# Sums of activations beside five column tiles, buffers allocated ahead, and a head's side work in one sequence, in a two-layer hybrid encoder

## The chip, the cores and the metric

The kernel runs on one core of one Trainium2 chip. The metric is the device time of one execution in microseconds (us); before the change the median of three runs is 1840.49 us (1838.7 to 1841.06). One more execution, taken by the hardware profiler, is the source of all rows quoted here.

A core has five engines that run side by side, each with its own queue in order: TensorE (PE; its weight loads are listed as PEld), VectorE (DVE), ScalarE (ACT), GpSimd (POOL) and SyncE (SP), which here issues most of the DMA transfers. TensorE writes to PSUM, eight banks of 512 float32 columns for each of 128 partitions; all else lies in SBUF or in DRAM.

## The reference

Sixteen learned meta tokens are put ahead of 512 tokens of width 2048, and two layers follow, each `h <- h + post_norm(mixer(pre_norm(h)))`. Layer 0 is softmax attention (16 query heads, 8 key heads, rotary positions). Layer 1, where the change lies, is gated linear attention (GLA) in two directions:

```python
def gla_mixer(h, w_in, gk_up, gk_bias, o_norm, w_out):
    ...
    proj = hp @ w_in
    q, k, v, g_out, lr_f, lr_b = jnp.split(proj, [s1, s2, s3, s4, s5], axis=-1)
    ...
    o_f = gla_chunked(q, k, v, log_gate(lr_f, gk_up[0], gk_bias[0]), strict=False)
    o_b = flip(gla_chunked(flip(q), flip(k), flip(v), ..., strict=True))
    o = (o_f + o_b).transpose(0, 2, 1, 3)[:, pad:]
    o = rmsnorm(o, o_norm).reshape(B, L, GLA_VALUE_DIM)
    return (o * jax.nn.silu(g_out[:, pad:])) @ w_out
```

It has 4 heads with keys of width 256 and values of width 512. `w_in` has the columns 0 to 1023 for q, 1024 to 2047 for k, 2048 to 4095 for v, 4096 to 6143 for the gate `g_out`, and 32 for the two low-rank decay gates. All is float32.

## The kernel before

**Three products for one.** Every float32 operand is split into a rounded part and the rest (`split`, L133 to L135: ScalarE casts to `hi`, VectorE subtracts to get `lo`), and a product is `hi*hi + hi*lo + lo*hi`: three matmuls (L157 to L159, L242 to L244). Activations lie as `uh`, `ul` (16 blocks of 128 rows, 528 columns, the tokens). `weights` (L146 on) loads a unit of 8 x 128 columns of weights into one of two `wraw` buffers through SP and splits it into one of three pairs `whi`, `wlo`. `project` takes two units, 16 blocks, and one or two column ranges of tokens (`HALVES` is twice 264, `REAL` is 512), accumulates in one of three PSUM banks of the tag `pp`, and hands the bank to an evacuation function.

**The order of the work** is that of the Python program, worked out as it runs: a small planner, `Clock`, has a time of its own that each projection block advances (`clk.step`) and a heap of side tasks with due times (`clk.after`, generators through `clk.drive`; `clk.finish` runs tasks until the named ones are done, whether or not projections go along). A framework below it adds the waits, assigns buffers, and moves instructions ahead where `high_priority` says so (weights by 400 instructions, quarters of `seven` by 600). Each engine then runs its list in that order.

**The stages around the change**, in order of time:

- *Residual and second norm.* After the attention layer, `residual` builds the new `h`, stores it in DRAM as `hf_d`, and writes the next layer's `uh`, `ul`. `second_norm` (L844) turns sums of squares of each token into a row `r1row` (one value for each token, the same in all partitions): for each of five groups of tokens it puts the values on a diagonal (`dg`, VectorE), multiplies by a matrix of ones (TensorE, `mrow`) and copies the result to its columns of `r1row` (ScalarE). `mrow` has one PSUM bank. Two `pp` banks hold the low-rank products `plr` until `r1row` has come.
- *Column tiles that go through DRAM.* `to_dram(n, c, ...)` (L858) projects 128 columns of `w_in`, multiplies by `r1row` and stores the tile in `kq_d[n]`: n = 0, 1 are the k tiles of head 0, n = 2 is its first q tile.
- *Sums of activations.* `combine` (L198) runs as a side task beside n = 1 and n = 2. For each k of 8 it loads block k and block k + 8 of `hf_d` into a buffer `x` of four times 264 columns, scales them by the norm's weights (L210, L211), forms the four combinations T1 to T4 by three subtractions (L212 to L214), and splits the result into `th`, `tl`. There are four buffers `x` (`quarters`).
- *Value tiles by seven products.* `seven` (L219) computes two value tiles of 128 columns with 7 half-size products in place of 8 (Strassen's scheme in Winograd's form): it loads four quarters of the weights (a11, a21, a22, a12) into buffers from the list `free`, forms three weight sums on VectorE (`sums`, L236), splits each operand, and takes products with quarters of `uh`, `ul` or with T1 to T4. The first product takes a11 itself, the second takes a weight sum and T2. The list starts with the four buffers of `combine`; the two `wraw` buffers come after them. It is called six times.
- *The four heads* (L1171 on). For each head h: q tiles are projected (`take_q`), beside `gates(h)` (decay gates) and `outputs(h - 1)` (the last head's output, which reads `vh`, `vl`, `gs`); when both are done, `scores(h)` starts with 15 slots, and `load_v(h)` (values from DRAM, five tiles through one buffer `vt`). Beside these run the k tiles of the next head and four gate tiles (`gate_tile`, L1152); in the last head two value tiles, which use the same buffer `vt`, and three gate tiles.

Of the kernel before, what the change touches and what calls it, by code (L numbers as in the profile page):

```python
# [10 lines left out]
F32 = mybir.dt.float32  # L11
# [3 lines left out]
ALU = mybir.AluOpType  # L15
# [4 lines left out]
P = 128  # L20
# [62 lines left out]
def hybrid_encoder(  # L83
# [9 lines left out]
    def pool(stack, name, bufs=1, **kw):  # L93
        return stack.enter_context(tc.tile_pool(name=name, bufs=bufs, reuse_waits="tile", **kw))
# [10 lines left out]
    hf_d = scratch.tile([KT, P, T], F32, name="hf_d")  # L105
    kq_d = scratch.tile([3, P, T], F32, name="kq_d")
    v_d = scratch.tile([5, P, D], F32, name="v_d")
# [16 lines left out]
    def col(i):  # L124
        return cols[:, i:i + 1]
# [11 lines left out]
    def rsqrt_inplace(t):  # L137
        A.activation(t, t, AF.Ln)
        A.activation(t, t, AF.Exp, scale=-0.5)
# [54 lines left out]

    T1, T3, T2, T4 = range(0, 4 * HALF, HALF)
    KH = KT // 2

    def combine(th, tl, xs, src, scale):  # L198

        def load(k):  # L200
            if k < KH:
                x = xs[k % len(xs)]
                nc.sync.dma_start(out=x[:, :T], in_=src[k])
                nc.sync.dma_start(out=x[:, T:T + HALF], in_=src[k + KH][:, HALF:])
                nc.sync.dma_start(out=x[:, T + HALF:], in_=src[k + KH][:, :HALF])
        for k in range(len(xs)):
            load(k)
        for k in range(KH):
            x = xs[k % len(xs)]
            A.activation(x[:, :T], x[:, :T], AF.Copy, scale=scale(k))  # L210
            A.activation(x[:, T:], x[:, T:], AF.Copy, scale=scale(k + KH))  # L211
            V.tensor_tensor(x[:, :T], x[:, HALF:HALF + T], x[:, :T], op=ALU.subtract)  # L212
            V.tensor_tensor(x[:, T2:T4], x[:, T2:T4], x[:, :HALF], op=ALU.subtract)
            V.tensor_tensor(x[:, T4:], x[:, T4:], x[:, T2:T4], op=ALU.subtract)  # L214
            split(th[:, k], tl[:, k], x)
            load(k + len(xs))
            yield 2.4
# [482 lines left out]
    la = ExitStack()  # L700
    yp = pool(la, "yp", 2)


# [140 lines left out]
    def second_norm():  # L844

        V.reduce_sum(r1col, s1, axis=AX.X)
        V.tensor_scalar(r1col, r1col, 1.0 / D, EPS, op0=ALU.mult, op1=ALU.add)
        rsqrt_inplace(r1col)
        for t, c, n in TOK:
            dg = t2.tile([P, P], F32, tag="dg", name="dg")  # L850
            V.tensor_scalar(dg, ident, r1col[:, t:t + 1], None, op0=ALU.mult)
            ps = ps_t.tile([P, 512], F32, tag="t", name="mrow")[:, :n]
            PE.matmul(ps, ones, dg[:, :n], start=True, stop=True)
            A.copy(r1row[:, c:c + n], ps)
        for ps, a, b in plr:
            V.tensor_tensor(lt[:, a:b], ps, r1row[:, a:b], op=ALU.mult)
# [26 lines left out]
    th, tl = [ta.tile([P, KH, 4 * HALF], F32R, name=f"t{w}") for w in "hl"]  # L883
    quarters = [ta.tile([P, 4 * HALF], F32, name=f"x{i}") for i in range(4)]

# [16 lines left out]
    to_dram(1, 1024 + P, 1.0, HALVES)  # L902
    to_dram(2, 0, 1.0 / 16, REAL)
    clk.finish(built)
    free = [q[:, :1024] for q in quarters]
    free += [wpool.tile([P, 1024], F32, tag="wraw", name="wraw", bufs=2) for _ in range(2)]
    for vc in range(2, 14, 2):
# [241 lines left out]
    def take_q(i, ps, a, b):  # L1149
        V.scalar_tensor_tensor(qf[:, i, a:b], ps, 1.0 / 16, r1row[:, a:b], op0=ALU.mult, op1=ALU.mult)  # L1150

    def gate_tile(h, i, last_k=None):  # L1152
        gr = g2.tile([P, SEQ], F32, tag="gr", name="gr", bufs=1)
        project(w_in1, 4096 + h * 512 + i * P, REAL,
                lambda ps, a, b: V.tensor_tensor(gr, ps, r1row[:, a:b], op=ALU.mult), last_k)
        sigmoid(gs[:, i], gr)
        V.scalar_tensor_tensor(gs[:, i], gs[:, i], col(ONORM + i), gr, op0=ALU.mult, op1=ALU.mult)

# [8 lines left out]
    def reload1(k):  # L1167
        split(uh[:, k, :SEQ], ul[:, k, :SEQ], slots1[k % len(slots1)])
        load_og1(k + len(slots1))

    for h in range(G_HEADS):  # L1171
        if h:
            side = [clk.drive(gates(h)), clk.drive(outputs(h - 1, 3.6))]
        else:
            sc = clk.drive(chain(gates(h), scores(h, 3.6)))
        for i in range(0 if h else 1, 2):
            project(w_in1, h * 256 + i * P, REAL, lambda ps, a, b: take_q(i, ps, a, b))
        if h:
            clk.finish(*side)
            sc = clk.drive(scores(h, 4.0))  # L1180
        vs = clk.drive(load_v(h))
        for i in range(2):
            if h < G_HEADS - 1:
                project(w_in1, 1024 + (h + 1) * 256 + i * P, HALVES, lambda ps, a, b: take_k(h + 1, i, ps, a, b))
            else:
                if not i:
                    clk.finish(vs)
                value_tile(h, 2 + i)
        for i in range(4):
            if h == G_HEADS - 1 and i == 3:  # L1190
# [10 lines left out]
            else:  # L1201
                gate_tile(h, i)
        clk.finish(sc, vs)
    clk.flush()
# [104 lines left out]
```

## Time and profile before

| | |
|---|---|
| median of three runs | 1840.49 us (1838.7 to 1841.06) |
| profiled execution | 1843.47 us, its span 1841.7 us |
| PE busy | 1787.2 us (97%) |
| PEld busy | 1677.4 us (91%) |
| DVE busy | 1064.3 us (58%) |
| ACT busy | 926.6 us (50%) |
| POOL busy | 198.1 us (11%) |
| mean granted clock of TensorE | 0.991 |

The span is the time from the first to the last instruction of the program; what lies around it is start and end. A row of instructions reads: line, engine, operation, what it writes `<-` what it reads, shapes and count, then busy time and mean length, then the idle time of that engine just before, and what ended it. In an order of time the first two columns are start and length. `SPq` stands for the queue of SyncE. Buffer numbers are left out in names, so `x` is any of the four buffers.

### The profile page before, as it was taken

To read this page: it belongs to the slowest core of one execution; us is meant where nothing else is said; L and a number is where in the kernel's file an instruction comes from. 1 tells how busy PE (TensorE), PEld (TensorE's weight loads), DVE (VectorE), ACT (ScalarE), POOL (GpSimd) and SP (SyncE) were. 2 spreads that over 40 slices of the span, in tenths; PEclk is the share of its full clock that TensorE was granted. 3 is DMA by queue.
4 is the path that set the end of the run, shared out by engine and by line. 5 is a ranking of instruction groups with operands and counts; after the bars stand their busy time and mean duration, and the time that the engine had idled before them with its cause. 6 is when DMAs were issued, how large, how long until landed. Compare 5 with 4: busy or idle time off the path is not lost.

```text
span 1841.7 us, 32124 instructions
## 1 busy us (share of the span) xinstructions
PE 1787.2 (97%) x12711; PEld 1677.4 (91%) x12711; DVE 1064.3 (58%) x2053; ACT 926.6 (50%) x1872; POOL 198.1 (11%) x253
## 2 busy tenths in 40 slices
PE   9999999999999999999998699999999999999998
PEld 8899999999999999999998599988888888888886
DVE  5776565656564747521273676567674856844224
ACT  4555444445454545533355544477574756843221
POOL 3211111111101111111131001100000000000000
PEclk9999999999999999999999899999999999999999
DMA  8322323232332332533464634433332332434323
GB/s 256 113 59 81 86 87 89 87 90 83 90 90 84 88 111 83 158 91 88 121 215 138 187 104 120 121 119 82 95 90 70 116 98 86 123 109 165 102 94 126
DMA packets 271928, 202.08 MB, mean 110 GB/s; under 512 B 10365, under 2 KB 242881, under 8 KB 271249
## 3 DMA queue, kind: packets, MB, share of 16 engines
q1 hardware_dynamic: 263824, 174.83, 32.7%
q0 software_dynamic: 7952, 25.20, 3.7%
q8 instruction: 100, 1.64, 0.4%
q14 instruction: 52, 0.42, 0.1%
HBM read 164.94 MB, written 28.56 MB: 105 GB/s over the span
## 4 chain that ended last, share of the span: by engine, by line
PE 59%; issue 32%; POOL 3%; DVE 3%; ACT 2%; DMA 1%; SPq 0%; POOLq 0%; DVEq 0%; ACTq 0%
PE pp L157 13%; PE pp L159 13%; PE pp L158 13%; PE f L1223 2%; PE f L1221 2%; PE f L1222 2%; PE pT L582 2%; POOL v_d L899 1%; PE s L563 1%; PE s L564 1%; PE s L565 1%; PE o L603 1%; PE o L602 1%; PE o L604 1%; ACT whi L134 1%
## 5 line engine op out<-in xcount | busy, mean ns | idle before, releaser
L157 PE MATMUL pp<-uh,whi 128*128 128x264 f32 (+1 forms) x2640 | 803.9, 305 | 0.3 <-ACT sq L303 0.3
L159 PE MATMUL pp<-uh,wlo 128*128 128x264 f32 (+1 forms) x2640 | 795.0, 301 | 0.3 <-POOL wlo L369 0.3
L158 PE MATMUL pp<-ul,whi 128*128 128x264 f32 (+1 forms) x2640 | 794.6, 301 | 0.2 <-DVE ul L430 0.2
L159 PEld LDWEIGHTS pp<-uh,wlo 128*128 128x128 f32 x2640 | 498.3, 189 | 17.4 <-POOL wlo L369 0.6
L157 PEld LDWEIGHTS pp<-uh,whi 128*128 128x128 f32 x2640 | 497.9, 189 | 16.9 <-ACT sq L303 0.5
L158 PEld LDWEIGHTS pp<-ul,whi 128*128 128x128 f32 x2640 | 498.9, 189 | 14.1 <-DVE ul L430 0.5
L135 DVE TENSOR_TENSOR wlo<-wraw,whi 128x1024 fp32r<-128x1024 f32 (+1 forms) x245 | 298.5, 1219 | 358.8 <-ACT whi L134 358.7
L134 ACT CAST whi<-wraw 128x1024 fp32r<-128x1024 f32 (+1 forms) x245 | 255.1, 1042 | 358.9 <-PE pp L158 207.4
L572 ACT ACTIVATE pn<-s,mx 128x528 f32<-128x528 f32 (+1 forms) x72 | 50.3, 698 | 88.5 <-DVE mx L569 67.2
L1223 PE MATMUL f<-whi,ul 128*128 128x512 f32 x192 | 75.6, 394 | 0.0
L1221 PE MATMUL f<-whi,uh 128*128 128x512 f32 x192 | 75.5, 393 | 0.0
L1222 PE MATMUL f<-wlo,uh 128*128 128x512 f32 x192 | 75.3, 392 | 0.0
L315 POOL TENSOR_TENSOR qw<-qw,cos 128x528 f32<-128x528 f32 x24 | 31.9, 1327 | 374.5 <-DMA qs<-qw 297.2
L568 DVE TENSOR_REDUCE mx<-s 128x1 f32<-128x528 f32 (+1 forms) x72 | 50.7, 705 | 18.7 <-PE s L565 17.6
L242 PE MATMUL pp<-th,whi 128*128 128x264 f32 x192 | 55.9, 291 | 5.3 <-ACT whi L134 5.1
L243 PE MATMUL pp<-tl,whi 128*128 128x264 f32 x192 | 55.4, 289 | 0.0
L244 PE MATMUL pp<-th,wlo 128*128 128x264 f32 x192 | 55.1, 288 | 0.0
L325 DVE TENSOR_TENSOR qw<-qw,qs 128x528 f32<-128x528 f32 x24 | 17.0, 706 | 61.2 <-POOL qs L316 61.2
L242 PE MATMUL pp<-uh,whi 128*128 128x264 f32 x144 | 42.5, 295 | 9.7 <-ACT whi L134 9.7
L587 DVE TENSOR_TENSOR pl<-pT,ph 128x512 fp32r<-128x512 f32 (+1 forms) x80 | 47.4, 592 | 4.8 <-ACT ph L586 3.8
L1100 POOL DMA_DIRECT2D og_d<-og x24 | 12.8, 541 | 346.6 <-DVE og L1098 346.4
L586 ACT CAST ph<-pT 128x512 fp32r<-128x512 f32 (+1 forms) x80 | 40.6, 507 | 16.6 <-PE pT L582 10.5
(373 smaller groups left out, 3358.0 us busy)
## 6 DMA issues: line engine op xcount, KB each, us to landing
wraw<-in_attn_w_in_dram SPq DMA_DIRECT2D x94, 512.0 KB, 4.0
wraw<-in_gla_w_in_dram SPq DMA_DIRECT2D x81, 512.0 KB, 3.9
wraw<-in_attn_w_out_dram SPq DMA_DIRECT2D x32, 512.0 KB, 3.9
wraw<-in_gla_w_out_dram SPq DMA_DIRECT2D x32, 512.0 KB, 3.8
x<-in_gla_w_in_dram SPq DMA_DIRECT2D x15, 512.0 KB, 4.2
qs<-qw SPq DMA_DIRECT2D x96, 66.0 KB, 3.0
h<-h_d SPq DMA_DIRECT2D x32, 132.0 KB, 3.3
hf_d<-h POOLq DMA_DIRECT2D x32, 132.0 KB, 3.7
```

What stands on the lines that cost most here:

```text
L134: A.copy(hi, src)
L135: V.tensor_tensor(lo, src, hi.bitcast(F32), op=ALU.subtract)
L157: PE.matmul(ps, wh, uh[:, k, a:b], start=first, stop=False)
L158: PE.matmul(ps, wh, ul[:, k, a:b], start=False, stop=False)
L159: PE.matmul(ps, wl, uh[:, k, a:b], start=False, stop=last)
L242: PE.matmul(ps, w[0][:, k], bh[:, k], start=k == 0, stop=False)
L243: PE.matmul(ps, w[0][:, k], bl[:, k], start=False, stop=False)
L244: PE.matmul(ps, w[1][:, k], bh[:, k], start=False, stop=k == KH - 1)
L568: V.reduce_max(mx, s, axis=AX.XY)
L1221: PE.matmul(ps, uh[:, k, ts], wh[:, kk], start=(k == 0), stop=False)
L1222: PE.matmul(ps, uh[:, k, ts], wl[:, kk], start=False, stop=False)
L1223: PE.matmul(ps, ul[:, k, ts], wh[:, kk], start=False, stop=(k == KT - 1))
```

## The change

Five edits go together:

- `combine` loads its two blocks with one transfer, in plain order, instead of three, and forms the combinations by one strided subtraction and two narrow ones. T2 and T4 change places.
- Two of the four buffers `x` are allocated in the pool `yp`, which is opened before the residual's stage; the other two stay where they were.
- `second_norm` puts four of its five products side by side in one bank and copies them with one instruction; the fifth product takes a `pp` bank. The diagonals take five buffers of the tag `h0` instead of two of their own.
- The first gate tiles of heads 1 and 2 are projected by `to_dram` (n = 3 and 4) right after the first q tile, before the sums are waited for, and kept in DRAM; `load_gate` brings each back in its head. The list `free` starts with the two `wraw` buffers.
- A head's side work is one generator, `head`: `gates`, then, when the q tiles and the last head's outputs are done, `scores` with slots of 3.4 (before: 3.6 in head 0 and 4.0 in the others), beside `load_v` and `load_gate`. In the last head `load_v` is no longer finished ahead of the value tiles.

```diff
--- before.py
+++ after.py
@@ -103,7 +103,7 @@
     og_d = scratch.tile([KT, P, T], F32, name="og_d")
     h1_d = scratch.tile([4, P, D], F32, name="h1_d")
     hf_d = scratch.tile([KT, P, T], F32, name="hf_d")
-    kq_d = scratch.tile([3, P, T], F32, name="kq_d")
+    kq_d = scratch.tile([6, P, T], F32, name="kq_d")
     v_d = scratch.tile([5, P, D], F32, name="v_d")
 
 
@@ -192,7 +192,7 @@
 
 
 
-    T1, T3, T2, T4 = range(0, 4 * HALF, HALF)
+    T1, T3, T4, T2 = range(0, 4 * HALF, HALF)
     KH = KT // 2
 
     def combine(th, tl, xs, src, scale):
@@ -200,18 +200,17 @@
         def load(k):
             if k < KH:
                 x = xs[k % len(xs)]
-                nc.sync.dma_start(out=x[:, :T], in_=src[k])
-                nc.sync.dma_start(out=x[:, T:T + HALF], in_=src[k + KH][:, HALF:])
-                nc.sync.dma_start(out=x[:, T + HALF:], in_=src[k + KH][:, :HALF])
+                nc.sync.dma_start(out=x.rearrange("p (j t) -> p j t", j=2), in_=src[k:k + KH + 1:KH].rearrange("j p t -> p j t"))
         for k in range(len(xs)):
             load(k)
         for k in range(KH):
             x = xs[k % len(xs)]
             A.activation(x[:, :T], x[:, :T], AF.Copy, scale=scale(k))
             A.activation(x[:, T:], x[:, T:], AF.Copy, scale=scale(k + KH))
-            V.tensor_tensor(x[:, :T], x[:, HALF:HALF + T], x[:, :T], op=ALU.subtract)
-            V.tensor_tensor(x[:, T2:T4], x[:, T2:T4], x[:, :HALF], op=ALU.subtract)
-            V.tensor_tensor(x[:, T4:], x[:, T4:], x[:, T2:T4], op=ALU.subtract)
+            q = x.rearrange("p (j t) -> p j t", j=4)
+            V.tensor_tensor(q[:, 0:2], q[:, 1::2], q[:, 0:2], op=ALU.subtract)
+            V.tensor_tensor(q[:, 3], q[:, 3], q[:, 0], op=ALU.subtract)
+            V.tensor_tensor(q[:, 2], q[:, 2], q[:, 3], op=ALU.subtract)
             split(th[:, k], tl[:, k], x)
             load(k + len(xs))
             yield 2.4
@@ -699,6 +698,7 @@
     lrs = [c1.tile([80, T], F32R, name=f"lr{d}") for d in range(2)]
     la = ExitStack()
     yp = pool(la, "yp", 2)
+    quarters = [yp.tile([P, 4 * HALF], F32, name=f"x{i}", bufs=1) for i in range(2)]
 
 
     tr = ExitStack()
@@ -846,12 +846,14 @@
         V.reduce_sum(r1col, s1, axis=AX.X)
         V.tensor_scalar(r1col, r1col, 1.0 / D, EPS, op0=ALU.mult, op1=ALU.add)
         rsqrt_inplace(r1col)
+        rows4 = ps_t.tile([P, 512], F32, tag="t", name="mrow")
         for t, c, n in TOK:
-            dg = t2.tile([P, P], F32, tag="dg", name="dg")
+            dg = t2.tile([P, HALF], F32, tag="h0", name="dg", bufs=5)[:, :P]
             V.tensor_scalar(dg, ident, r1col[:, t:t + 1], None, op0=ALU.mult)
-            ps = ps_t.tile([P, 512], F32, tag="t", name="mrow")[:, :n]
+            ps = rows4[:, c:c + n] if t < 4 else ps_p.tile([P, 512], F32, tag="pp", name="mrow")[:, :n]
             PE.matmul(ps, ones, dg[:, :n], start=True, stop=True)
-            A.copy(r1row[:, c:c + n], ps)
+        A.copy(r1row[:, :SEQ], rows4)
+        A.copy(r1row[:, SEQ:], ps)
         for ps, a, b in plr:
             V.tensor_tensor(lt[:, a:b], ps, r1row[:, a:b], op=ALU.mult)
 
@@ -881,7 +883,7 @@
     sa = pool(la, "sa", 2)
     ps_v = pool(la, "ps_v", 2, space=PSUM)
     th, tl = [ta.tile([P, KH, 4 * HALF], F32R, name=f"t{w}") for w in "hl"]
-    quarters = [ta.tile([P, 4 * HALF], F32, name=f"x{i}") for i in range(4)]
+    quarters += [ta.tile([P, 4 * HALF], F32, name=f"x{i}") for i in range(2, 4)]
 
     def token_rows(ys, vc):
 
@@ -901,9 +903,11 @@
     clk.after(1.0, lambda ys=ys: token_rows(ys, 0))
     to_dram(1, 1024 + P, 1.0, HALVES)
     to_dram(2, 0, 1.0 / 16, REAL)
+    for n, h in ((3, 1), (4, 2)):
+        to_dram(n, 4096 + h * 512, 1.0, REAL)
     clk.finish(built)
-    free = [q[:, :1024] for q in quarters]
-    free += [wpool.tile([P, 1024], F32, tag="wraw", name="wraw", bufs=2) for _ in range(2)]
+    free = [wpool.tile([P, 1024], F32, tag="wraw", name="wraw", bufs=2) for _ in range(2)]
+    free += [q[:, :1024] for q in quarters]
     for vc in range(2, 14, 2):
         ys = y_tiles()
         free = seven(w_in1, 2048 + vc * P, ys, th, tl, free)
@@ -1149,12 +1153,21 @@
     def take_q(i, ps, a, b):
         V.scalar_tensor_tensor(qf[:, i, a:b], ps, 1.0 / 16, r1row[:, a:b], op0=ALU.mult, op1=ALU.mult)
 
+    def gated(h, i, gr):
+        sigmoid(gs[:, i], gr)
+        V.scalar_tensor_tensor(gs[:, i], gs[:, i], col(ONORM + i), gr, op0=ALU.mult, op1=ALU.mult)
+
     def gate_tile(h, i, last_k=None):
         gr = g2.tile([P, SEQ], F32, tag="gr", name="gr", bufs=1)
         project(w_in1, 4096 + h * 512 + i * P, REAL,
                 lambda ps, a, b: V.tensor_tensor(gr, ps, r1row[:, a:b], op=ALU.mult), last_k)
-        sigmoid(gs[:, i], gr)
-        V.scalar_tensor_tensor(gs[:, i], gs[:, i], col(ONORM + i), gr, op0=ALU.mult, op1=ALU.mult)
+        gated(h, i, gr)
+
+    def load_gate(h):
+        gr = g2.tile([P, SEQ], F32, tag="gr", name="gr", bufs=1)
+        nc.sync.dma_start(out=gr, in_=kq_d[2 + h][:, :SEQ])
+        yield 4.0
+        gated(h, 0, gr)
 
 
     EARLY1 = 5
@@ -1168,25 +1181,32 @@
         split(uh[:, k, :SEQ], ul[:, k, :SEQ], slots1[k % len(slots1)])
         load_og1(k + len(slots1))
 
+    def head(h, before):
+
+        yield from gates(h)
+        while not (before["done"] and have["q"]):
+            yield 0.5
+        side = [clk.drive(load_v(h))]
+        if 0 < h < 3:
+            side.append(clk.drive(load_gate(h)))
+        yield from scores(h, 3.4)
+        while not all(s["done"] for s in side):
+            yield 0.5
+
     for h in range(G_HEADS):
-        if h:
-            side = [clk.drive(gates(h)), clk.drive(outputs(h - 1, 3.6))]
-        else:
-            sc = clk.drive(chain(gates(h), scores(h, 3.6)))
+        have = {"q": False}
+        before = clk.drive(outputs(h - 1, 3.6)) if h else {"done": True}
+        sc = clk.drive(head(h, before))
         for i in range(0 if h else 1, 2):
             project(w_in1, h * 256 + i * P, REAL, lambda ps, a, b: take_q(i, ps, a, b))
-        if h:
-            clk.finish(*side)
-            sc = clk.drive(scores(h, 4.0))
-        vs = clk.drive(load_v(h))
+        have["q"] = True
+        clk.finish(*([before] if h else []))
         for i in range(2):
             if h < G_HEADS - 1:
                 project(w_in1, 1024 + (h + 1) * 256 + i * P, HALVES, lambda ps, a, b: take_k(h + 1, i, ps, a, b))
             else:
-                if not i:
-                    clk.finish(vs)
                 value_tile(h, 2 + i)
-        for i in range(4):
+        for i in range(1 if 0 < h < 3 else 0, 4):
             if h == G_HEADS - 1 and i == 3:
                 clk.finish(sc)
                 slots1 = [kf[:, i, :SEQ] for kf in kfs for i in range(2)] + [qf[:, 0], qf[:, 1]]
@@ -1200,7 +1220,7 @@
                 gate_tile(h, i, lambda k: reload1(k - 8) if 8 <= k < 8 + EARLY1 else None)
             else:
                 gate_tile(h, i)
-        clk.finish(sc, vs)
+        clk.finish(sc)
     clk.flush()
     pv = clk.drive(outputs(G_HEADS - 1, 3.6))
```

## The prediction

> **What bounds the kernel now.** I read the page's busy times and its forty slices first, then stretches of time around the one slice where TensorE (PE) falls off, then the instructions there in order of time.
>
> ```profile
> span 1841.7 us, 32124 instructions
> PE 1787.2 (97%) x12711; PEld 1677.4 (91%) x12711; DVE 1064.3 (58%) x2053; ACT 926.6 (50%) x1872; POOL 198.1 (11%) x253
> PE   9999999999999999999998699999999999999998
> ```
>
> TensorE issues nearly all the time. The change neither adds nor removes a projection, so time can only come out of the places where TensorE stands still or runs slowly; slices 23 and 24 hold the largest. Columns below: stretch, PE, PEld, VectorE (DVE), ScalarE (ACT) and POOL busy, granted clock, DMA.
>
> ```profile
> 1001.00:1007.00 6.00, 3.97 (x22) 2.75 (x20) 2.46 (x9) 2.17 (x9) 0.00 (x0) 0.93 0.01 3
> 1007.00:1014.00 7.00, 7.00 (x48) 6.86 (x48) 1.66 (x2) 2.77 (x7) 2.14 (x4) 0.81 0.13 46
> ...
> 1038.60:1048.30 9.70, 0.01 (x1) 0.00 (x0) 8.03 (x16) 5.94 (x9) 0.54 (x1) 0.77 0.79 239
> 1048.30:1054.30 6.00, 5.55 (x24) 5.21 (x24) 3.54 (x3) 1.90 (x2) 0.00 (x0) 0.53 0.33 91
> 1054.50:1059.60 5.10, 0.01 (x1) 0.01 (x1) 3.70 (x4) 1.48 (x3) 0.00 (x0) 0.78 0.00 0
> 1059.60:1066.00 6.40, 6.26 (x33) 5.95 (x34) 5.04 (x5) 2.55 (x3) 0.00 (x0) 0.64 0.46 120
> 1066.00:1081.00 15.00, 15.00 (x125) 15.00 (x125) 12.47 (x15) 5.59 (x6) 0.00 (x0) 1.00 0.33 91
> ```
>
> The last row is the full rate: 15.00/125 = 0.12 us per matmul of 264 columns. Against it the stretch from 1038.6 loses 9.7 us idle, then 6.0 - 24 x 0.12 = 3.1 us to a clock of 0.53, then 5.1 us idle, then 6.4 - 33 x 0.12 = 2.4 us at 0.64. **Together 20.3 us**, in the hand-over from the last `to_dram` to the first `seven`. What ended it:
>
> ```profile
> 996.41 1.98 SPq L790 DMA_DIRECT2D h_d<-hb  x2
> 1013.35 0.38 SPq L152 DMA_DIRECT2D wraw<-in_gla_w_in_dram  x1
> 1016.27 0.38 SPq L223 DMA_DIRECT2D wraw<-in_gla_w_in_dram  x1
> 1016.76 0.64 SPq L203 DMA_DIRECT2D x<-hf_d  x1
> ...
> 1027.55 0.40 PE L158 MATMUL pp<-ul,whi 128*128 128x512 f32 x1
> 1027.78 0.40 PE L159 MATMUL pp<-uh,wlo 128*128 128x512 f32 x1
> ...
> 1048.30 0.59 PE L242 MATMUL pp<-uh,whi 128*128 128x264 f32 x1 [9.69 <-ACT whi L134]
> ...
> 1047.21 1.04 ACT L134 CAST whi<-x 128x1024 fp32r<-128x1024 f32 x1 [2.55 <-DMA x<-in_gla_w_in_dram]
> ...
> 1012.10 1.23 DVE L135 TENSOR_TENSOR wlo<-wraw,whi 128x1024 fp32r<-128x1024 f32 x1 [4.47 <-ACT whi L134]
> ...
> 1040.89 0.68 DVE L863 SCALAR_TENSOR_TENSOR y<-pp,r1row 128x512 f32<-128x512 f32 x1
> ...
> 1049.43 2.42 DVE L135 TENSOR_TENSOR tl<-x,th 128x1056 fp32r<-128x1056 f32 x2
> 1054.72 3.74 DVE L236 TENSOR_TENSOR x<-x,x 128x1024 f32<-128x1024 f32 x3 [2.87 <-issue]
> 1059.57 3.50 DVE L135 TENSOR_TENSOR wlo<-x,whi 128x1024 fp32r<-128x1024 f32 x3 [1.11 <-ACT whi L134]
> ```
>
> The first weights (a11) lie in an `x` buffer that the sums of activations used until shortly before, so their load came late. The sums end at 1051.85 (1049.43 + 2.42), the other quarters land after them, three weight sums (L236) follow, and TensorE restarts at 1059.6. It had run dry at 1038.6.
>
> **The change, part by part.**
>
> *Two gate tiles beside the sums.* `to_dram(3)` and `to_dram(4)` are the first gate tiles of heads 1 and 2, taken out of the head loop. Each is 48 matmuls of 512 columns, 0.23 us apart (1027.55 to 1027.78): 11.0 us, together 22.1. The work is moved, not added: TensorE now has work until 1038.6 + 22.1 = 1060.7, and then the first product of `seven` (24 x 0.12 = 2.9) until 1063.6. The first weights must be split by the first, the weight sums by the second. Is VectorE done by then? Its groups from 1015 to 1060:
>
> ```profile
> L135 DVE TENSOR_TENSOR tl<-x,th 128x1056 fp32r<-128x1056 f32 x8 | 9.8, 1253 | 1.7 <-ACT th L134 1.7
> L212 DVE TENSOR_TENSOR x<-x 128x528 f32<-128x528 f32 x8 | 5.5, 703 | 2.6 <-ACT x L211 2.6
> L236 DVE TENSOR_TENSOR x<-x,x 128x1024 f32<-128x1024 f32 x3 | 3.7, 1224 | 2.9 <-issue 2.9
> L213 DVE TENSOR_TENSOR x<-x 128x264 f32<-128x264 f32 x8 | 3.3, 428 | 0.1
> L214 DVE TENSOR_TENSOR x<-x 128x264 f32<-128x264 f32 x8 | 3.3, 428 | 0.1
> L135 DVE TENSOR_TENSOR wlo<-wraw,whi 128x1024 fp32r<-128x1024 f32 x2 | 2.4, 1222 | 0.5 <-ACT whi L134 0.5
> ```
>
> The two tiles add four weight splits (4 x 1.22) and two evacuations (the 512-column one at 1040.89 took 0.68), 6.3 us. Even if the sums started no earlier, their end moves from 1051.85 to 1058.2; 3.74 of weight sums and about 1.1 to the cast bring 1063.0, just before 1063.6. Lower bound of what is left: 0. Upper bound: each added instruction also costs its length again in waiting between ScalarE and VectorE: 1064.5 + 4.8 = 1069.3, so 5.7 us late. I take 1.5, near the lower end, because of the next two edits. Gain here: 20.3 - 1.5 = **18.8 us** (bounds 20.3 and, with one slow stretch of 2.4 to 3.1 behind a long gap, 11.5).
>
> The row that sets the slow stretches is the clock of 0.53 behind 9.7 us of idleness. The Trainium skill ("TensorE: Matmul & The Clock Gate", section "What's actually happening") says that TensorE drops to half clock after an idle window of about 3.4 us and comes back after about 3.4 us of work; the trace agrees in kind (0.53, and 0.64 after 5.1 us), and prices it higher, 2.4 to 3.1 us against 3.4/2 = 1.7. By that rule a rest of 1.5 us draws no slow stretch at all and one of 5.7 us adds 1.7.
>
> *Buffers ahead, weights in other buffers.* Two of the four `x` buffers live in a pool opened before the stage of the residual, so their loads need not wait for its tiles (first load at 1016.76). SyncE (SP) issued nothing from 998.4 to 1013.35, and VectorE stood 4.47 us idle before 1012.10, so two of the eight sums can be brought to L214 early: 2 x (0.70 + 0.43 + 0.43) = 3.1 us. a11 and a21 go to the `wraw` buffers, which come free when the last split of `to_dram(4)` is done, about one 5.5 us half tile ahead of 1060.7, instead of behind the sums. Priced inside the 18.8.
>
> *One load instead of three per sum, one strided subtraction.* 16 issues of 0.4 us leave SP; same bytes, same 528 + 264 + 264 columns on VectorE. 0; it matters only if SP were last, which no wait there shows.
>
> *Norm's row in one bank.* The row's chain, in the groups from 1001 to 1007, behind a copy of a whole bank:
>
> ```profile
> 995.38 0.61 ACT L789 COPY hb<-ht 128x512 f32<-128x512 f32 x1
> ```
>
> ```profile
> L853 PE MATMUL mrow<-dg,ones 128*128 128x128 f32 (+1 forms) x10 | 2.6, 338 | 2.0 <-DVE dg L851 1.1 <-ACT r1row L854 1.0
> L851 DVE TENSOR_SCALAR dg<-ident,r1col 128x128 f32<-128x128 f32 x5 | 1.3, 286 | 2.0 <-PE mrow L853 1.5 <-ACT r1col L139 0.5
> L854 ACT COPY r1row<-mrow 128x128 f32<-128x128 f32 (+1 forms) x5 | 1.2, 247 | 3.3 <-PE mrow L853 3.3
> ```
>
> Five turns of matmul, copy, next become five matmuls and two copies. TensorE's 1.0 us behind r1row and some of VectorE's 1.5 go. The single copy of 512 columns costs 0.61 by the copy at 995.38 instead of 0.25, and the fifth matmul needs a bank of the three `pp`, of which two are held by `plr`: it may wait for that copy and the product at L856. Between -2.5 and +1.0; I take **-1.0**. The slow clock after it (7.0 - 48 x 0.12 = 1.2 us) stays.
> *Heads in sequence.* By the program's own clock `gates` takes 20.8 us and the q tiles 20.76, so `scores` starts as before. It has 15 slots: 51 us at 3.4 instead of 60 at 4.0, and its cover (two k tiles, gate tiles) falls from 63 to 53 in heads 1 and 2. Head 3 no longer runs `load_v` to its end ahead of its value tiles, which had pushed five slots together. ScalarE's occupancy decides:
>
> ```profile
> 1222.00:1262.00 40.00, 39.18 (x221) 33.44 (x222) 35.88 (x70) 39.11 (x97) 0.00 (x0) 1.00 0.32 87
> 1337.00:1417.00 80.00, 80.00 (x462) 69.94 (x461) 49.27 (x83) 51.20 (x106) 0.00 (x0) 1.00 0.31 84
> ...
> 1556.00:1602.00 46.00, 43.86 (x310) 40.11 (x311) 41.21 (x87) 42.71 (x113) 2.13 (x4) 1.00 0.36 101
> ```
>
> Head 1's stage (second row) has ScalarE at 51.2 of 80; some 11 us shorter it is at about 74%: room. Head 3 (third row) lost 46.0 - 43.86 = 2.1 us of TensorE at 93%; that can be regained. Head 0 (first row) is full at 39.11 of 40 and now gets `load_v` there and slots 6% shorter; it can lose 2 to 5, as head 3 did at such a density. `load_gate` adds a 256 KB load, a sigmoid and a product per head, off the path. I take **+1.0** (bounds -2 and +8).
>
> **Sum.** The profiled execution took 1843.47 us (span 1841.7 and 1.8 around it), 3.0 above the median of 1840.49. 1843.5 - 18.8 - 1.0 + 1.0 = 1824.7 for such an execution, hence **1821.7** beside the median; I say 1821.5.
>
> **Rivals.**
>
> *A. The wait comes back as weights behind the sums.* The order of VectorE's work puts sums, splits and evacuations in each other's way; the rest is 5.7 us and its slow stretch: 1821.5 + 4.2 + 2.4 to 3.1 = 1828 to 1829. For it: VectorE at 8.03 of 9.70 while TensorE waited. Against: 22.1 us of cover for 6.3 us of new work.
>
> *B. ScalarE sets the pace of the heads.* All 8 us of that bound: 1828.5. For: 39.11 of 40. Against: 51.20 of 80.
>
> Two rows for the next one: SP's waits at `load_v` (total, times, longest) and how long weights take to land.
>
> ```profile
> SPq L1137 <- DVE vl L135: 13.7, 8, 3.4
> ```
>
> ```profile
> wraw<-in_gla_w_in_dram SPq DMA_DIRECT2D x81, 512.0 KB, 3.9
> ```
>
> *C. Slower: SP stands still in head 3.* `load_v` and the value tiles share one `vt` buffer; formerly the one ended before the other began. If a `load_v` transfer reaches the head of SP's queue while a value tile holds `vt`, all later weights stand behind it: 48 x 0.12 = 5.8 us of second half plus 6 us to the last transposes, stretched by score matmuls to about 14, then 3.9 landing, 1.04 cast, 1.22 split; less one unit in hand (5.8). Per tile 14 us, for two 29: **1850**. It decides when the hold outlasts the weights in hand. Against: these loads' waits were short, 3.4 at most on VectorE's splits.
>
> *D. It does not do what it says.* a11's load still stands behind other loads in SP's queue, and the 20 us reappear after 1060: 1840. Against: `wraw` is turned over every half tile.
>
> *E. More than forecast.* The rest is 0, the norm saves 2.5, heads save their 2: 1843.5 - 20.3 - 2.5 - 2 - 3.0 = 1816, and some lower if the heads' many small waits close too.
>
> **How the numbers follow.** Chances: forecast 0.54, A 0.15, B 0.12, C 0.05, D 0.04, E 0.10. The range is 1812 to 1833: it takes in E, A and B (and A with half of B) and leaves out C, D and A and B in full together. About 0.2% (3.7 us) is what a measurement of this kernel can tell from no change: faster 0.89, same 0.05 (D, and A and B together at their worst), slower 0.06 (C and what I do not see).
>
> **What would show it.** Right: the TensorE gap before the first product of `seven` under 3 us, granted clock near 1 through that stretch, first loads of `x` before 1013, heads 1 and 2 about 11 us shorter each. Wrong: a wait of `pp` on `whi` above 5 us there (A), waits of `ss` on `hq` of several us per head (B), an idle stretch in head 3's value tiles with SP waiting at the load of `vt` (C). If the total is right but the heads gained or lost more than 5 us, the sum was right by accident.

## The result, and the profile after

The changed kernel takes **1820.61 us** (median of 4 runs, 1816.72 to 1823.16) against 1840.78 for the kernel before: a ratio of **0.989**, 95% interval 0.987 to 0.991. Timed again later it took 1821.5 us, ratio 0.9896 (0.9883 to 0.991). Forecast were 1821.5 us and a range of 1812 to 1833. The profiled execution took 1819.71 us.

The page's span, TensorE (PE) row and forty slices, after:

```profile
span 1818.0 us, 32105 instructions
PE 1777.5 (98%) x12711; PEld 1670.0 (92%) x12711; DVE 1063.0 (58%) x2053; ACT 924.8 (51%) x1869; POOL 199.3 (11%) x255
PE   8999999999999999999999999999999999999998
```

As many matmuls, and no slice below 90% between the first and the last. The stretch that had lost 20.3 us (columns as in the prediction: PE, PEld, DVE, ACT, POOL busy, granted clock, DMA):

```profile
1025.00:1035.00 10.00, 10.00 (x45) 8.11 (x44) 10.00 (x17) 7.13 (x9) 0.58 (x1) 1.00 0.88 249
1035.00:1045.00 10.00, 10.00 (x45) 8.11 (x44) 8.18 (x10) 6.29 (x7) 0.54 (x1) 1.00 0.71 202
1045.00:1057.30 12.30, 12.30 (x55) 9.98 (x54) 5.52 (x7) 2.10 (x2) 0.54 (x1) 1.00 0.43 130
1057.30:1060.30 3.00, 3.00 (x26) 2.95 (x26) 2.96 (x4) 1.05 (x1) 0.00 (x0) 1.00 0.00 0
1060.30:1066.00 5.70, 5.70 (x50) 5.70 (x49) 3.91 (x4) 2.47 (x3) 0.54 (x1) 1.00 0.71 197
```

TensorE is busy all of the time at a clock of 1.00. In the order of time:

```profile
968.25 0.37 SPq L203 DMA_DIRECT2D x<-hf_d  x1
...
1013.06 1.08 ACT L134 CAST th<-x 128x1056 fp32r<-128x1056 f32 x1
...
1042.70 1.26 DVE L135 TENSOR_TENSOR tl<-x,th 128x1056 fp32r<-128x1056 f32 x1 [0.60 <-ACT th L134]
...
1054.70 1.22 DVE L235 TENSOR_TENSOR wraw<-x,wraw 128x1024 f32<-128x1024 f32 x1
...
1056.03 1.05 ACT L134 CAST whi<-wraw 128x1024 fp32r<-128x1024 f32 x1 [8.50 <-DVE wraw L235]
...
1057.13 0.39 PE L159 MATMUL pp<-uh,wlo 128*128 128x512 f32 x1
1057.36 0.28 PE L241 MATMUL pp<-uh,whi 128*128 128x264 f32 x1
```

The first `x` load leaves at 968, the sums end at 1043.96 (before: 1051.85), the last weight sum that the second product needs ends at 1055.9, and the last gate tile's matmul at 1057.13 is followed by the first of `seven` after 0.23 us, the usual distance. Nothing is waited for: the second product's weights are split by 1058.34, 1.9 us ahead of the end of the first (1057.36 + 24 x 0.12).

Where the 23.7 us between the two spans lie, by marked instructions (the first product of the norm's row, the last product with T1 to T4, the first decay product of head 0, and the first sum of an output's squares after each head, `sso`; as an example the rows of the heads' first and last mark, before, then after):

```profile
1206.95 0.36 PE L968 MATMUL pz<-lr,ups 80*128 80x264 f32 x1 [0.62 <-DVE ups L958]
...
1657.68 0.59 PE L1091 MATMUL sso<-acc,ones 128*128 128x256 f32 x2
```

```profile
1206.34 0.36 PE L972 MATMUL pz<-lr,ups 80*128 80x264 f32 x1 [0.82 <-DVE ups L962]
...
1634.08 0.59 PE L1095 MATMUL sso<-acc,ones 128*128 128x256 f32 x2
```

| part of the span | before | after | work moved | net |
|---|---|---|---|---|
| start to the norm's row | 1003.0 | 1000.6 | | -2.4 |
| norm's row, sums, value tiles | 181.2 | 183.3 | +22.1 | -20.0 |
| to the first decay product | 22.8 | 22.5 | | -0.4 |
| heads | 450.7 | 427.7 | -22.1 | -0.9 |
| rest | 184.1 | 183.9 | | -0.1 |

The first 2.4 us are not a gain that the edits are known to bring: in the fourteen traces of this study the first transposes of the new `h`, behind an attention layer that the edits do not touch, start anywhere from 933.0 to 939.9 us. This scatter, and that of the granted clock around the norm's row (last section), is in all times below.

To set the runs side by side I also sum TensorE's **loss**: over neighbouring matmuls, how much later the next one starts than it usually does behind that line and shape (idle and slow clock together). Between 1014 and 1075 us it is 21.5 us before and 0.3 after.

### The profile page after: what moved, and what is told of

Read it like the earlier page. It is cut to its first block, busy times and chain, and to the rows that moved or that the text cites. A ratio compares the mean times of both kernels' runs of the same rounds, so it can differ in the third digit from the quotient of the medians.

```text
span 1818.0 us, 32105 instructions
## 1 busy us (share of the span) xinstructions
PE 1777.5 (98%) x12711; PEld 1670.0 (92%) x12711; DVE 1063.0 (58%) x2053; ACT 924.8 (51%) x1869; POOL 199.3 (11%) x255
## 4 chain that ended last, share of the span: by engine, by line
PE 62%; issue 31%; POOL 3%; DVE 2%; DMA 1%; ACT 1%; SPq 0%; POOLq 0%; DVEq 0%; ACTq 0%
PE pp L157 14%; PE pp L159 14%; PE pp L158 14%; PE f L1243 2%; PE f L1241 2%; PE f L1242 2%; PE pT L581 2%; POOL v_d L901 1%; PE s L562 1%; PE s L563 1%; PE s L564 1%; PE o L602 1%; PE o L601 1%; PE o L603 1%; POOL hf_d L754 1%
## 5 line engine op out<-in xcount | busy, mean ns | idle before, releaser
L134 ACT CAST whi<-x 128x1024 fp32r<-128x1024 f32 x27 | 28.3, 1048 | 43.3 <-PE pp L242 21.4
```

Of the source, the lines that this page charges most:

```text
L134: A.copy(hi, src)
```

## The experiments

All kernels compute the whole result; each was timed in five rounds beside the kernel before.

### The changed kernel again

> The changed kernel once more, on the chip of the three others, to stand beside them: 1818 to 1823 by its four runs so far.

Measured: 1821.50 us (1820.38 to 1823.92), the yardstick for the runs below; its loss from 1014 to 1075 is 0.6 us.

### The cover alone

```diff
...
+    for n, h in ((3, 1), (4, 2)):
+        to_dram(n, 4096 + h * 512, 1.0, REAL)
...
-            sc = clk.drive(scores(h, 4.0))
+            sc = clk.drive(scores(h, 3.4 if h < 3 else 4.0))
+        lg = clk.drive(load_gate(h)) if 0 < h < 3 else sc
...
-        for i in range(4):
+        for i in range(1 if 0 < h < 3 else 0, 4):
```

> The kernel before with one part alone: the first gate tiles of heads 1 and 2 are projected after the first q tile and brought back in their heads (slots of 3.4 in heads 1 and 2, where the cover shrinks; all else as before: three loads per sum, x buffers allocated late, a11 in an x buffer, norm and heads as before). Theory 'cover': 22.1 us of projections stand where TensorE stood still or ran slowly for 20.3 us, so this part alone brings nearly all: 1821 to 1825. Rival 'order of buffers': the wait is a transfer into an x buffer that comes free too late, and with more work ahead of it on VectorE it only moves back: 1832 to 1840.

Measured: 1827.85 us, ratio 0.9932 (0.9918 to 0.9945). Both numbers missed, the theory of the hand-over held: the loss from 1014 to 1075 is 0.7 us with three loads per sum, late buffers and a11 in an `x` buffer. Of the other 6 to 7 us to the changed kernel the two profiles show 4.9 in the heads (432.6 against 427.7) and 2.2 around the norm's row (both below). In this run the sums end 50.8 us after the norm row's first product, against 48.9 before: the two tiles push them back by 2.0 us, not by the 6.3 of their added instructions.

### No cover

```diff
-    for n, h in ((3, 1), (4, 2)):
-        to_dram(n, 4096 + h * 512, 1.0, REAL)
...
-        for i in range(1 if 0 < h < 3 else 0, 4):
+        for i in range(4):
```

> The changed kernel with the two gate tiles back in their heads (no tile through DRAM for them), all else as changed. Theory 'cover': TensorE runs dry near 1036, the sums end near 1038.5 without the extra splits, the quarter for the weight sums lands near 1041, sums and cast end near 1046; TensorE loses about 7 us and 2.4 us of slow clock: 1828 to 1832. Rival 'order of buffers': nothing is lost, 1820 to 1823.

Measured: 1826.34 us, ratio 0.9922 (0.991 to 0.9935). The hand-over is as expected: a gap, then half the clock.

```profile
1038.70:1044.60 5.90, 0.12 (x1) 0.00 (x0) 5.90 (x7) 2.47 (x4) 0.54 (x1) 0.90 0.46 133
1044.60:1048.00 3.40, 3.18 (x13) 2.88 (x14) 3.40 (x4) 1.92 (x3) 0.00 (x0) 0.50 0.55 149
```

VectorE works through all 5.90 us of the gap: the weight sums are last. The loss is 9.9 us. The time is 1.7 us below the expected range; the heads, 2 us shorter than before (448.7 against 450.7), are of that size.

### Early buffers and order of weights alone

```diff
+    quarters = [yp.tile([P, 4 * HALF], F32, name=f"x{i}", bufs=1) for i in range(2)]
...
-    free = [q[:, :1024] for q in quarters]
-    free += [wpool.tile([P, 1024], F32, tag="wraw", name="wraw", bufs=2) for _ in range(2)]
+    free = [wpool.tile([P, 1024], F32, tag="wraw", name="wraw", bufs=2) for _ in range(2)]
+    free += [q[:, :1024] for q in quarters]
```

> The kernel before with two of the four x buffers allocated ahead of the residual's stage and the first weights in the two wraw buffers, nothing else (no cover, no norm, no single load, heads as before). Without the two tiles the changed kernel kept 9.9 us of the 21.5 us that TensorE loses between 1014 and 1075. Theory: the buffers did that; 11 to 13 us are left there and the time is 1829 to 1833. Rival: the norm's row, which alone brought 4.5 us, and the single load had a large part in it; 15 us or more are left, 1833 to 1838.

Measured: 1828.74 us, ratio 0.9934 (0.992 to 0.9947); loss from 1014 to 1075 9.3 us, 1.7 us less than the theory's lower end, so the buffers and the order did more than I gave them. The first gap (9.69 before) is gone; the second one, for the weight sums, stays:

```profile
1046.21 0.59 PE L242 MATMUL pp<-th,whi 128*128 128x264 f32 x1 [5.82 <-ACT whi L134]
```

The single transfer and the strided subtraction have no run of their own. The pairs of runs that differ by them, among others, show nothing that they bring to the hand-over: 9.3 us are lost here without them and 9.9 in the run without cover, which has them.

### Cover with late buffers

```diff
-    quarters = [yp.tile([P, 4 * HALF], F32, name=f"x{i}", bufs=1) for i in range(2)]
...
+    quarters = [ta.tile([P, 4 * HALF], F32, name=f"x{i}") for i in range(4)]
...
+    free = [q[:, :1024] for q in quarters]
+    free += [wpool.tile([P, 1024], F32, tag="wraw", name="wraw", bufs=2) for _ in range(2)]
```

> The changed kernel with the four x buffers allocated late again and the first weights in x buffers again; cover, norm, single load and heads as changed. Theory 'cover': 22.1 us of cover nearly suffice without it, the rest is 0 to 6 us: 1820 to 1826. Rival: the buffers are needed, TensorE waits 5 us or more and runs slowly behind it: 1827 to 1835.

Measured: 1823.69 us, ratio 0.9906 (0.9889 to 0.9923), an interval that overlaps the changed kernel's. The hand-over loses 0.6 us. So the two parts stand in for each other: cover alone takes 20.8 of the 21.5 us, buffers and order alone 12.2, both with the rest 21.2.

### One tile instead of two

```diff
-    for n, h in ((3, 1), (4, 2)):
+    for n, h in ((3, 1),):
```

> The changed kernel with one of the two gate tiles moved (head 1's), head 2's back in its head. Theory: with buffers and norm as changed 9.9 us are open without a tile, one tile is 11.0 us, so one is enough: TensorE loses under 2 us between 1014 and 1064 and the time is 1819 to 1822, as with two. Rival: the tile's own weight splits and its evacuation on VectorE (3.1 us) push the sums back, 3 us or more of waiting and a slow clock stay: 1823 to 1827.

Measured: 1821.01 us, ratio 0.9892 (0.9878 to 0.9906): as with two tiles. From 1014 to 1064 TensorE loses 1.1 us. With early buffers 11 us of cover suffice for the hand-over; the second tile is reserve.

### The norm's row alone

```diff
+        rows4 = ps_t.tile([P, 512], F32, tag="t", name="mrow")
...
-            ps = ps_t.tile([P, 512], F32, tag="t", name="mrow")[:, :n]
+            ps = rows4[:, c:c + n] if t < 4 else ps_p.tile([P, 512], F32, tag="pp", name="mrow")[:, :n]
             PE.matmul(ps, ones, dg[:, :n], start=True, stop=True)
-            A.copy(r1row[:, c:c + n], ps)
+        A.copy(r1row[:, :SEQ], rows4)
+        A.copy(r1row[:, SEQ:], ps)
```

> The kernel before with the norm's row in one bank alone. Theory: 1 us less, 1839 to 1841, hardly to be told from no change in time, so the stretch from the first product of the row to the restart of the projections is read in the trace: 3.8 us before (1002.97 to 1006.8), 3.0 to 3.8 here. Rival: the fifth product's wait for a bank gives all of it back: 3.8 or more.

Measured: 1836.30 us, ratio **0.9978** (0.9968 to 0.9988): 4.1 us by the ratio (2.2 to 5.9), four times what I gave it. The row itself, first before, then in the changed kernel:

```profile
1002.97 0.49 PE L853 MATMUL mrow<-dg,ones 128*128 128x128 f32 x2 [1.07 <-DVE dg L851]
...
1006.34 0.61 PE L853 MATMUL mrow<-dg,ones 128*128 128x16 f32 x2
```

```profile
1000.58 1.16 PE L854 MATMUL mrow<-dg,ones 128*128 128x128 f32 x8 [1.29 <-DVE dg L852]
1002.88 0.52 PE L854 MATMUL mrow<-dg,ones 128*128 128x16 f32 x2 [1.03 <-DVE r L858]
1003.33 1.14 PE L873 MATMUL lrf<-r,fold 128*64 128x264 f32 x2
1004.41 0.59 PE L157 MATMUL pp<-uh,whi 128*128 128x264 f32 x1
```

The fifth product starts 2.30 us after the first instead of 3.37, although it waits 1.03 us for a bank. The projections restart no sooner (3.83 us after the first product against 3.82), but only because the first half of the low-rank product `lrf` (1.08 us), which came one projection half later before, now stands ahead of them. So I compare the same work, the 161 matmuls from the row's first product to the first one of 512 columns: 24.35 us before, 23.41 in the changed kernel, 23.45 with this edit alone, each with 3.41 us at half clock in it. The row gives 0.9 us.

The larger part is not where I looked: the loss from 1014 to 1075 is 18.6 us, 2.9 less than before. The first load of `x` leaves 10.7 us after the row's first product (1000.34) instead of 13.8, and the hand-over's first gap shrinks from 9.69 to 7.21 us:

```profile
1011.03 0.63 SPq L203 DMA_DIRECT2D x<-hf_d  x1
...
1013.49 0.38 SPq L223 DMA_DIRECT2D wraw<-in_gla_w_in_dram  x1
```

```profile
1042.31 0.59 PE L242 MATMUL pp<-uh,whi 128*128 128x264 f32 x1 [7.21 <-ACT whi L134]
```

In the kernel before these two loads stand the other way round in SyncE's queue (1016.27 and 1016.76 in the prediction's rows): the load of weights waits 2.4 us there for a split on VectorE, and `x` behind it. Why the order changed is not shown. My guess is `lrf`, which reads tiles of the residual's stage: its first half is issued 2.6 us after the row's first product instead of 11.0. With cover this second part has nothing to shorten (cover alone, with the row as before, loses 0.7 us there); the row's own gain stays.

### The fifth product in another bank

```diff
-            ps = ... else ps_p.tile([P, 512], F32, tag="pp", name="mrow")[:, :n]
+            ps = ... else ps_g.tile([P, 512], F32, name="g00")[:, :n]
```

> The changed kernel with the fifth product of the norm's row in a bank of the group that has just been copied out, instead of one of the three projection banks. In the changed kernel's trace TensorE stands 1.2 us ahead of that product. Theory: the wait was for the projection bank and goes: about 1 us less, 1819 to 1821, and no gap above 0.5 us ahead of the fifth product. Rival: the wait was for the diagonal or for the copy, and stays.

Measured: 1821.80 us, ratio 0.9898 (0.9883 to 0.9914). The wait for the bank is gone from the trace, and the fifth product starts 1.6 us after the first instead of 2.3, so it was the bank; the time is not lower. The order around it changed with it: both halves of `lrf` are issued later again (1012.4 and 1017.1 instead of 1003.3 and 1011.4). A wait was removed, and no gain shows; 1 us would be within the interval.

### The heads

```diff
-            side = [clk.drive(gates(h)), clk.drive(outputs(h - 1, 3.6))]
...
-            sc = clk.drive(scores(h, 4.0))
-        vs = clk.drive(load_v(h))
...
+        before = clk.drive(outputs(h - 1, 3.6)) if h else {"done": True}
+        sc = clk.drive(head(h, before))
...
-                if not i:
-                    clk.finish(vs)
```

> The kernel before with the new sequence of a head alone (slots of 3.4, values loaded beside the scores, no forced end of the value load in head 3), gate tiles all in the heads. Theory: TensorE waits little in the heads before (about 20 us over 440 us, in many small pieces), the sequence moves them by 1 us: 1838 to 1842. Rival 'heads': the sequence closes the pieces, 1833 to 1837.

Measured: 1839.33 us, ratio 0.9997 (0.9988 to 1.0007): no change that the times can tell. In the trace the heads are 2.2 us shorter (448.6 against 450.7).

The reverse, the changed kernel with the old loop:

```diff
-        sc = clk.drive(head(h, before))
+            side = [clk.drive(gates(h)), clk.drive(outputs(h - 1, 3.6))]
...
+            sc = clk.drive(scores(h, 4.0))
+        lg = clk.drive(load_gate(h)) if 0 < h < 3 else sc
```

> The changed kernel with the loop over the heads as before (scores after the q tiles with slots of 4.0, value load driven apart and ended ahead of head 3's value tiles), the two gate tiles still ahead and brought back in heads 1 and 2. By the program's own clock 60 us of slots then meet 53 us of cover in heads 1 and 2, so some 7 us of scores are issued without projections between them at the end of each. Theory: TensorE waits for ScalarE there, up to 2 x 3 us, and head 3 loses 2 us as before: 1823 to 1829. Rival 'the sequence does nothing': 1820 to 1822.

Measured: 1824.84 us, ratio 0.9916 (0.9901 to 0.993), 3 to 4 us above the changed kernel, with intervals that overlap. The lengths of the heads between marks tell where:

| kernel | head 0 | head 1 | head 2 | head 3 |
|---|---|---|---|---|
| before | 98.5 | 117.2 | 117.2 | 117.9 |
| before with new heads | 98.9 | 117.8 | 117.0 | 114.9 |
| changed with old heads | 98.5 | 107.1 | 107.1 | 117.9 |
| cover alone | 99.6 | 107.7 | 107.3 | 118.0 |
| changed | 98.7 | 107.1 | 106.9 | 115.0 |
| changed, again | 98.8 | 107.2 | 107.4 | 114.8 |

By these lengths the new sequence is worth 2.9 us in head 3, and this is there in every profile that has it (the run with later sums of squares, below, apart); it moves the other heads by 0.7 us at most. Heads 1 and 2 do not mind the sequence: at slots of 4.0 they have the same length, though 60 us of slots meet 53 of cover. I had expected 2 x 3 us there; no such wait shows. In the changed kernel each lost 11.0 us of work and got 10.1 to 10.2 us shorter.

### Reads that come too early

The changed kernel's waits of TensorE from 1075 to 1640 (in total, times, longest):

```profile
PE vps L896 <- DVE y L248: 3.6, 5, 1.1
PE sso L1095 <- ACT z L973: 2.1, 3, 0.7
PE sso L1095 <- DVE acc L1092: 2.1, 2, 1.1
PE sm L1012 <- DVE lq L135: 2.1, 3, 1.0
```

The first of them is dearer than it was in the kernel before:

```profile
PE vps L894 <- DVE y L249: 1.6, 5, 0.8
```

The five profiles without cover wait 1.2 to 1.8 us there; the seven that have one tile or two and these due times wait 2.5 to 4.6. So with cover some 2 us are lost again later on, which I had overlooked; what delays these sums on VectorE is not shown. The second row is another kind of wait: `sso` and the decay products `pz` share one PSUM bank (tag `m`), and `sso` waits until ScalarE has copied `z` out of it.

```diff
-        clk.after(1.0, lambda ys=ys, vc=vc: token_rows(ys, vc))
+        clk.after(2.5, lambda ys=ys, vc=vc: token_rows(ys, vc))
...
+            yield 2.0
             ps = ps_m.tile([P, 512], F32, tag="m", name="sso")[:, :256]
-            yield 1.0
             PE.matmul(ps, ones, acc[:, :256], start=True, stop=True)
```

> The changed kernel with the transposes of the value tiles due 2.5 us after the last product instead of 1.0 us, and the product that sums the squares of an output due 2.0 us after its inputs are issued instead of 1.0. In the changed kernel TensorE waits 3.6 us at the first (for the sum of a product) and 4.6 us at the second. Theory: work that can run stands in the queue behind them, so 5 to 8 us go: 1813 to 1816. Rival: the waits move to what is issued next to them: 1819 to 1822.

Measured: 1828.53 us, ratio 0.9924 (0.9911 to 0.9937): 7 us slower than the changed kernel. The transposes' wait fell to 0.5 us, the others grew:

```profile
PE sso L1095 <- ACT z L973: 7.6, 6, 2.4
PE sm L1011 <- ACT hq L134: 6.3, 3, 3.0
```

The edit also moves the allocation of the bank behind the `yield`, and `sso` now waits for a copy out of the shared bank six times instead of three. And with each output 2 us longer by the program's own clock, the scores, which wait for the outputs, start late: their first products come 34 to 36 us after the mark that begins the head in heads 1 to 3, in the changed kernel 31 to 32. Which of the two parts of the edit costs more was not tried. So the last run moved the transposes alone:

```diff
-        clk.after(1.0, lambda ys=ys, vc=vc: token_rows(ys, vc))
+        clk.after(2.5, lambda ys=ys, vc=vc: token_rows(ys, vc))
```

> The changed kernel with the transposes of the value tiles alone due 2.5 us after the last product instead of 1.0 us; the sums of squares of the outputs as changed. In the run that moved both, TensorE's loss between 1075 and 1190 was 3.9 us instead of 6.3, and the heads lost more. Theory: the 2.4 us stay without the loss in the heads: 1817 to 1820, a ratio to the kernel before of 0.987 to 0.989, which the intervals may not tell from the changed kernel's 0.989; in the trace 4 us or less lost between 1075 and 1190 and no more than before in the heads. Rival: the loss in the heads came from the transposes too: 1823 or more.

Measured: **1817.35 us**, ratio 0.9878 (0.9862 to 0.9895). The loss from 1075 to 1190 is 3.5 us (changed kernel 6.3, and 7.1 in its second profile), the heads are as long as in the changed kernel (428.0 against 427.7), and the waits that are left do not include the products' sums:

```profile
PE sso L1095 <- ACT z L973: 2.2, 3, 0.7
PE sso L1095 <- DVE acc L1092: 2.1, 2, 1.1
PE sm L1012 <- DVE lq L135: 2.1, 3, 1.0
```

By the medians it is 3 to 4 us faster than the changed kernel, by the loss 2.8 (its profile has no half clock around the norm's row either, which is scatter); the two intervals overlap.

## Why the prediction was right, point by point

**The hand-over: -18.8.** Right in place, and the size came out at the upper end: the loss fell by 21.2 us, from 21.5 to 0.3. The rest that I left there, 1.5 us, was 0.3. Some 2 us of it came back at the value tiles' transposes (3.6 us of waiting instead of 1.6), a cost of the cover that is no term of the sum. With the norm's row, 0.9, this gives the 20.0 us of the table; that -18.8 and -1.0 add to nearly the same is in part luck. The reason was wrong in one point: I held the rest to be small *because of* the early buffers and the order of the weights. Those are not needed (0.6 us lost without them). The bound worked out without them, 1063.0 against 1063.6, was the better reading, and still too careful, since the sums moved by 2.0 us and not by 6.3: the two tiles are cover enough even for sums that start late.

**The norm's row: -1.0.** Right where it was priced: 0.9 us for the same work, with the fifth product's wait for a bank, named as a risk, inside it (1.03). What it left out is the 2.9 us that the edit alone brings to the hand-over through the order of loads in SyncE's queue; beside the cover this path has nothing to shorten.

**The heads: +1.0.** They gave -0.9. The price for head 0, 2 to 5 us at full ScalarE, did not come:

```profile
1222.00:1262.00 40.00, 39.53 (x225) 33.36 (x224) 35.91 (x70) 38.83 (x96) 0.00 (x0) 1.00 0.31 87
1333.00:1410.00 77.00, 77.00 (x474) 68.68 (x472) 49.64 (x90) 52.44 (x115) 0.00 (x0) 1.00 0.30 84
...
1545.00:1595.00 50.00, 49.78 (x321) 44.03 (x321) 39.13 (x79) 43.37 (x111) 0.00 (x0) 1.00 0.38 108
```

ScalarE stays near full in head 0 (38.83 of 40) and TensorE waits no more than it did (39.53 busy, before 39.18). Head 1's stage is at 52.44 of 77, 68%. Head 3 lost 0.2 us in 50 where it had lost 2.1 in 46: the gain that I took for possible, 2.1, came as 2.9. The term's sign was wrong: the loss in head 0 that it was made of did not come. What heads 1 and 2 keep, 0.9 us each, I had not priced.

**Rival C** showed in the trace as a wait, not as a loss. In head 3 SyncE stood at a load of `vt` until a value tile's transpose:

```profile
SPq L1141 <- PE vpm L1125: 4.9, 1, 4.9
```

Once, 4.9 us, shorter than the 5.8 us of weights in hand: the point from which it decides was not reached. Rivals A and D are excluded by the hand-over's 0.3 us, B by the heads' -0.9 (the waits of `ss` on `hq`, B's sign, are 0.4 us in all). E's low end did not come: the norm gave 0.9 of its 2.5, the heads 0.9 of their 2, and the transposes took 2 back.

**The sum.** Forecast for the profiled kind of execution 1824.7, measured 1819.71; of the 5.0 us between, 2.4 lie ahead of the change and 1.9 in the heads. Beside the median 1821.5 was forecast, and 1820.61 and 1821.5 were measured.

## What to carry to other kernels

Where the engine that sets the end runs dry between two stages, independent work of the same engine put there pays at once and leaves little to other repairs of the same gap: cover took 20.8 us, earlier buffers 12.2, the norm 2.9, and all of them 21.2. So ask of each edit what it is worth beside the others. Where a single edit seems to gain too much, look at what moved in the other queues. And compare stretches of the same work: a stretch between two marks can keep its length because other work moved into it.

A read that is issued before its data is there costs an in-order engine its wait each time (0.2 to 1.1 us at each of the five transposes), and a later due time can recover it (3 us here by the trace); but a due time that also moves the start of a chain can cost more than the wait (7 us).

## What the runs showed of the hardware that was not expected

I had tied TensorE's slow clock to a long gap: 0.53 behind 9.7 us. Around the norm's row it comes without one, before (0.81 from 1007 to 1014, in the prediction's rows) as in the changed kernel:

```profile
998.30:1000.60 2.30, 1.01 (x10) 0.77 (x9) 0.71 (x4) 1.09 (x4) 0.00 (x0) 1.00 0.05 13
1000.60:1002.90 2.30, 1.27 (x10) 1.03 (x10) 1.22 (x6) 0.58 (x1) 0.00 (x0) 1.00 0.00 0
1002.90:1004.40 1.50, 1.50 (x4) 0.68 (x4) 0.69 (x2) 0.91 (x3) 0.12 (x1) 0.53 0.00 0
1004.40:1006.00 1.60, 1.60 (x8) 1.59 (x8) 0.42 (x1) 0.98 (x3) 0.95 (x2) 0.50 0.25 87
```

The longest gap is 1.29 us (ahead of the first product of the row); over 4.6 us TensorE was half busy (2.28 us), and the clock fell to 0.5 for 3.41 us, from 1003.00 to 1006.41. A single gap of 2.29 us at the transposes, in the run with one tile, drew nothing:

```profile
1071.00:1073.50 2.50, 0.21 (x3) 0.01 (x1) 2.47 (x4) 1.26 (x3) 1.07 (x2) 1.00 0.10 38
1073.50:1077.00 3.50, 3.50 (x30) 3.46 (x31) 1.07 (x1) 0.86 (x1) 0.00 (x0) 1.00 0.44 128
```

A gap of the same length in the same place (2.31 us), in the changed kernel with the old heads, drew 3.41 us of half clock:

```profile
1080.60:1084.00 3.40, 1.33 (x12) 1.29 (x13) 3.11 (x4) 0.83 (x3) 1.07 (x2) 1.00 0.22 77
1084.00:1087.40 3.40, 3.40 (x18) 3.40 (x17) 0.08 (x1) 1.16 (x2) 0.00 (x0) 0.50 0.58 159
```

The clock records of the fourteen traces tell these apart. Within each trace all changes of the granted clock lie on a grid of 3.41 us (in the changed kernel at 951.80, 955.21, 1003.00 and 1006.41, that is 1, 14 and 1 steps apart). I took TensorE's busy share of every step of that grid from 100 to 1800 us that ran at full clock, 6908 of them. All 36 steps that were busy for 45% or less were followed by half clock; of the 50 from 46 to 67%, 7 were; of the rest, none. So a gap counts by what it leaves of the step that it falls into: 39% in the run with the old heads (1080.6 to 1084.0), while in the run with one tile a line of the grid cuts the gap at 1071.7 and leaves 85% ahead of it and 48% behind.

This is also why the stretch behind the norm's row scatters: it drew 0, 3.41 or 6.83 us of half clock. With the new row the same 161 matmuls took 21.9 us (four profiles), 23.4 (three) or 24.8 (two), with the old one 24.4 at 3.41 (one) and 25.5 to 25.6 at 6.83 (three): 0.7 to 0.9 us for the edit at the same clock. The run with the fifth product in another bank, which has another order there, is left out.

So the rule of the Trainium skill that the prediction used ("TensorE: Matmul & The Clock Gate", section "What's actually happening": half clock after an idle window of about 3.4 us) has the length of the step as these traces show it, 3.41 us. But the step need not be idle: a few microseconds of sparse work, with no gap of that length, were enough. Nor is every rest under 3.4 us safe, as the prediction took it: 2.31 us drew the slow clock in one run.
